# Two transformer blocks on one core: the first stage's order, a shift applied behind a transpose, and two attention heads moved ahead of a projection

## The chip, the core and the metric

The kernel runs as one launch on one core of a Trainium2 chip. The core has five instruction streams, each executed in its own order: TensorE (PE, matrix products and transposes, with PEld for its weight loads), VectorE (DVE), ScalarE (ACT), GpSimd (POOL) and SyncE (SP, which here only issues transfers). Transfers (DMA) are issued by an engine into a queue and moved by 16 shared DMA engines. The metric is the device time of one execution in microseconds (us); lower is better.

## The reference

Two blocks follow each other on 512 tokens of width 1024, in 32-bit floats. What the change touches is the first block's mixer and the start and the second attention of the second block's mixer:

```python
# first block
h = rmsnorm(x, norm1_g[l])
proj = h @ w_in[l]
qa, ka, va, iq, ik, iw, qb, kb, vb, g_lr, r_gate = jnp.split(proj, split_points, axis=-1)
...
o_a = dsa_attention(qa, ka, va, iq..., ik, iw, rel_bias)   # an index score picks 128 keys a query
...
o_b = gla_chunked(...)                                      # gated linear attention
x = x + jnp.concatenate([o_a, o_b], axis=-1) @ w_out[l]
x = x + hier_moe(rmsnorm(x, norm2_g[l]), ...)               # 32 experts
# second block: c gives a shift and a scale, h = rms_norm(x) * g * (1 + scale) + shift
...
proj = h @ w_in
o_mla = causal_block_attention(q_mla, k_mla, v_mla, ...)
o_fox = causal_block_attention(heads(fq), heads(fk), heads(fv), ..., cum_log_f)
...
# then 64 routed experts and a shared one
```

The six vectors of shift, scale and gate come from `silu(c) @ w_mod + b_mod`, `c` being a vector of 1024 numbers and `w_mod` 1024 x 6144. They depend on nothing that the first block computes.

## The kernel before

Tokens lie in four tiles of 128 (`t` or `i`). A product in 32 bits is made of three passes: an operand is split into a high part and a rest (`xh`, `xl`, and `wh`, `wl` for weights, lines 136 and 137), and lines 108 to 110 multiply high by high, high by rest, rest by high. So each chunk of a weight (0.5 MB, `w`, line 130) is loaded by SP, split by ACT (`wh`) and POOL (`wl`), and then read by PE.

A scheduler decides the order of each engine's instructions when the program is built, from the order of the code, from priorities and from hints such as `issue_after`; on the chip that order is fixed.

**First stage** (`phase_a`, the first 330 us). Projections of the first block are made one after another: the index part (`ev_d`), q (`qT`), k (`kT`), then the values (`va`), then those of the linear attention. For q and k each tile is copied out by ACT (line 344, with a square for the norm in line 346), normalised by DVE (line 354, k only), transposed by PE (line 358) and copied back by ACT (line 359). `select(i)` makes the mask of the best keys for tile i: PE makes index scores (`ix`, line 307), ACT takes their positive part (`rl`, line 309), DVE sums them (line 313) and then takes 16 rounds of eight maxima each (lines 319 and 321). The attention heads come in a `front` (scores `qk` in line 379, DVE softmax steps in lines 387 and 389) and a `back` (line 406 transposes, line 415 values), the back `LAG` = 2 pairs of heads behind the front.

Beside this runs `phase_mod`, a generator: the first two of the six vectors of the second block (j = 0 the shift, j = 1 the scale) are computed on PE from `mw`, 1 MB pieces of `w_mod` in two buffers. Each of the four pieces of a j gives eight small products (line 1439); then ACT copies the sum (`macc`) and PE folds it (line 1445), DVE adds the bias (line 1446) and the result is stored in memory (`modD`). `ccol` is silu(c). The bias table of the attention (`brs`, 2.5 MB, issued on ACT's queue) is read back in pieces (`toep`, line 383) on SP's queue.

**Turn to the second block** (`phase_c`, from 630 us). For each half (512 columns) of each token tile DVE computes `h` = x · rs · gs (line 1503), POOL adds the shift, held as a row repeated on 128 partitions (line 1504), PE transposes it (line 1507, `xt`), ACT copies the high part `xh` (line 116) and DVE makes the rest `xl` (line 117). The first projection starts on these parts.

**Second attention of the second block** (`attention(qF, kF, ...)`). Its values `vF` are projected first, then its heads start.

After the first stage and between the mixers stand the expert layers, whose weights (1 MB pieces `wg`, `wu`, `wd`, line 801) are loaded by SP into buffers that come free as the work goes on.

Of the kernel before, what the change touches and what calls it, by code (L numbers as in the profile page):

```python
# [19 lines left out]
NT = 4  # L20
KD = 8
# [33 lines left out]
class K:  # L55
# [84 lines left out]
    def proj(self, pool, xh, xl, segs, evac, kd=KD, wb=2):  # L140

        width = sum(hi - lo for _, lo, hi in segs)
        banks = [self.pbank("pr") for _ in range(NT)]
        for h in range(0, kd, 2):
            nk = min(2, kd - h)
            wh, wl = self.weights(pool, segs, h, nk, 512, wb)
            for t in range(NT):
                ts = slice(t * 128, (t + 1) * 128)
                for j in range(nk):
                    self.mm3(banks[t][:, :width], rows(xh, h + j)[:, ts], rows(xl, h + j)[:, ts], wh[:, j, :width],  # L150
                             wl[:, j, :width], h + j == 0, h + j == kd - 1)
        for t in range(NT):
            evac(t, banks[t])
# [23 lines left out]
ML = 12  # L177
MA = (0, 0, 16, 0)


def phase_a(k, side):
# [321 lines left out]
    def step(n):  # L503
        for _ in range(n):
            next(mod, None)
    k.proj(po, xh, xl, [(w_in, 1536, 1832), (w_in, 2856, 2872)], ev_d)
    step(MA[0])
# [5 lines left out]
    step(MA[1])  # L513
    select(2)
    k.proj(po, xh, xl, [(w_in, 512, 1024)], ev_qk(kT, False))
    with tc.issue_after(act), tc.issue_after(dve), tc.issue_after(k.wloads[ML]):
        step(MA[2])
    select(3)
    k.proj(po, xh, xl, [(w_in, 1024, 1536)], lambda t, b: nc.scalar.activation(va[:, t, :], b, AF.Copy))
    step(MA[3])  # L520
    heads = [(i, hp) for i in range(NT) for hp in range(4)]
    for n in range(len(heads) + LAG):
        if n < len(heads):
            front(*heads[n])
        if n >= LAG:
            i, hp = heads[n - LAG]
            for r in range(2):
                back(i, 2 * hp + r)
    step(16)
# [884 lines left out]
def phase_mod(k, ctx):  # L1414
# [5 lines left out]
    c, _ = mod_col(k, pool)  # L1420
# [5 lines left out]
    nc.gpsimd.tensor_copy(sel, s2[:, :, None].to_broadcast([128, 2, 32]))  # L1426
    wv = I["w_mod_2"][0].rearrange("(p k) n -> p k n", p=128)
# [29 lines left out]
def rows_c(k):  # L1457
# [12 lines left out]
    def load(after):  # L1470
        with k.tc.issue_after(after):
            got.extend(row(k, p, s, n, "r", 3, k.nc.sync) for s, n in
                       ((k.modD[D:2 * D], "gs"), (k.modD[:D], "sh"), (k.I["g_mix_norm_2"][0], "gr")))
# [12 lines left out]
def phase_c(k, rctx, rp, rows):  # L1486
# [12 lines left out]
    for t in range(NT):  # L1499
        h = e.tile([128, D], F32, name="h", bufs=2)  # L1500
        for q in range(2):
            c = slice(q * 512, (q + 1) * 512)
            nc.vector.scalar_tensor_tensor(h[:, c], k.xres[:, t, c], rs4[:, t:t + 1], gs[:, c], op0=ALU.mult, op1=ALU.mult)
            nc.gpsimd.tensor_add(h[:, c], h[:, c], sh[:, c])
            b = k.bank("xt")
            for j in range(4):
                nc.tensor.transpose(b[:, j * 128:(j + 1) * 128], h[:, (4 * q + j) * 128:(4 * q + j + 1) * 128], ident)
            ts = slice(t * 128, (t + 1) * 128)
            k.split(xs[q][0][:, :, ts], xs[q][1][:, :, ts], b.rearrange("p (k s) -> p k s", k=4))
# [182 lines left out]

    def attention(q, kt, v, oT, kd):
        heads = [(i, h) for i in range(NT) for h in range(8)]
        for n in range(len(heads) + 2):
            if n < len(heads):
                front(q, kt, kd, *heads[n])
            if n >= 2:
                back(v, oT, *heads[n - 2])


    oM = a.tile([128, 4, 2, S], F32R, name="oM")
    attention(qM, kM, vM, oM, 96)
    vF = p.tile([128, NT, 512], F32, tag="v", name="vF", bufs=2)
# [329 lines left out]
```

## Time and profile before

| | |
|---|---|
| median of 3 runs (range) | 1698.6 us (1694.95 to 1703.54) |
| the profiled execution | 1696.1 us |
| its span in the trace | 1694.3 us |
| mean granted TensorE clock | 0.963 of full speed |
| PE busy | 1556.0 us, 92% |
| DVE busy | 969.3 us, 57% |
| ACT busy | 540.5 us, 32% |
| POOL busy | 359.0 us, 21% |

Busy shares are averages over stages that have different limits. PE at 92% leaves 138 us in which it waits; where those lie, and what ends each of them, is what the trace has to say.

### The profile page before, as it was taken

What the parts mean: (1) busy time and instruction counts of PE and PEld (TensorE: products, weight loads), DVE (VectorE), ACT (ScalarE), POOL (GpSimd) and SP (SyncE); (2) the same over time, 40 slices, a digit from 0 to 9 for tenths busy, and PEclk for the clock granted to TensorE, in tenths of its full rate; (3) what the DMA queues carried; (4) which work ended last, traced back from release to release, by engine and by line L of the source; (5) the groups of instructions that cost most, each with busy time, mean ns of one, the idle gap of its engine ahead of it and who ended that gap; (6) DMA issues with size and microseconds to landing.
All of it is one profiled execution on the core that took longest, in us unless ns stands there. A gap on an engine that the chain in (4) does not pass through costs nothing.

```text
span 1694.3 us, 28618 instructions
## 1 busy us (share of the span) xinstructions
PE 1556.0 (92%) x10917; PEld 1063.8 (63%) x10917; DVE 969.3 (57%) x2195; ACT 540.5 (32%) x1068; POOL 359.0 (21%) x296
## 2 busy tenths in 40 slices
PE   6789998987999877899999998999999999999996
PEld 5565556774665446675657776865666666666663
DVE  4492875853655346637454535455656656656656
ACT  4431876431211123545562222311112112112112
POOL 2332561012101105331104442113111111011000
PEclk9898999997999997999999999899999999999998
DMA  4526234467999963233005836758999999999961
GB/s 150 179 62 215 74 111 153 190 228 276 417 416 416 418 261 104 71 92 112 26 1 177 255 120 226 290 195 321 378 409 381 400 407 416 422 415 421 415 265 63
DMA packets 103311, 421.30 MB, mean 249 GB/s; under 512 B 22420, under 2 KB 29050, under 8 KB 65796
## 3 DMA queue, kind: packets, MB, share of 16 engines
q1 hardware_dynamic: 81984, 389.77, 59.8%
q0 software_dynamic: 9968, 19.04, 3.1%
q10 hardware_dynamic: 11220, 10.63, 1.9%
q8 instruction: 87, 1.43, 0.3%
q14 instruction: 52, 0.43, 0.1%
HBM read 420.51 MB, written 9.21 MB: 254 GB/s over the span
## 4 chain that ended last, share of the span: by engine, by line
PE 47%; DVE 4%; DMA 3%; POOL 1%; ACT 1%; issue 1%; SPq 0%; DVEq 0%; ACTq 0%; POOLq 0%
PE g L972 8%; PE u L972 8%; PE sc L1050 7%; PE y L996 7%; PE qk L1660 2%; PE ob L1688 2%; DMA mw<-in_w_mod_dram 2%; PE xT L937 2%; PE pt L110 2%; PE pt L109 1%; PE pt L108 1%; PE pt L1680 1%; DVE macc L1399 1%; DMA w<-in_w_in_dram 1%; PE wo L109 1%
## 5 line engine op out<-in xcount | busy, mean ns | idle before, releaser
L137 POOL TENSOR_TENSOR wl<-w,wh 128x1024 fp32r<-128x1024 f32 (+4 forms) x72 | 167.3, 2325 | 384.5 <-ACT wh L136 373.7
L1051 DVE TENSOR_TENSOR xres<-xres,sc 128x512 f32<-128x512 f32 x368 | 224.5, 682 | 4.2 <-PE sc L1050 1.0
L972 PE MATMUL u<-wu,xT 128*32 128x256 f32 (+2 forms) x2240 | 180.3, 388 | 11.9 <-DMA wu<-in_w_exp_up_dram 8.4
L972 PE MATMUL g<-wg,xT 128*32 128x256 f32 (+2 forms) x2240 | 177.2, 383 | 1.3 <-SPq L1143 0.8
L914 POOL DMA_INDIRECT xg<-hD,ii x46 | 46.2, 1004 | 609.3 <-issue 504.4
L996 PE MATMUL y<-wd,hT 128*32 128x512 f32 (+2 forms) x1120 | 167.6, 596 | 0.0
L972 PEld LDWEIGHTS u<-wu,xT 128*32 128x32 f32 (+2 forms) x2240 | 119.9, 121 | 62.1 <-DMA wu<-in_w_exp_up_dram 10.3
L972 PEld LDWEIGHTS g<-wg,xT 128*32 128x32 f32 (+2 forms) x2240 | 104.5, 119 | 85.0 <-issue 33.4
L978 DVE SCALAR_TENSOR_TENSOR hid<-u,gc,hid 128x256 f32<-128x256 f32 x46 | 22.3, 484 | 236.1 <-PE u L972 236.1
L136 ACT ACTIVATE wh<-w 128x1024 fp32r<-128x1024 f32 (+4 forms) x88 | 89.8, 1021 | 196.6 <-PE pt L109 74.2
L1050 PE MATMUL sc<-yh,st 128*128 128x512 f32 x368 | 152.2, 416 | 0.0
L1050 PE MATMUL sc<-yl,st 128*128 128x512 f32 x368 | 144.4, 395 | 0.1
L986 ACT ACTIVATE hT<-hT 128x256 f32<-128x256 f32 x46 | 17.7, 385 | 300.3 <-PE hT L983 300.3
L109 PE MATMUL pr<-wl,xh 128*128 128x512 f32 (+2 forms) x256 | 104.5, 408 | 6.0 <-POOL wl L137 6.0
L116 ACT ACTIVATE yh<-y 128x512 fp32r<-128x512 f32 x92 | 55.0, 597 | 163.0 <-DVE y L1004 110.7
L108 PE MATMUL pr<-wh,xh 128*128 128x512 f32 (+2 forms) x256 | 103.3, 408 | 0.3 <-ACT xh L116 0.3
L996 PEld LDWEIGHTS y<-wd,hT 128*32 128x32 f32 (+2 forms) x1120 | 46.6, 118 | 90.7 <-issue 88.3
L110 PE MATMUL pr<-wh,xl 128*128 128x512 f32 (+2 forms) x256 | 102.9, 403 | 0.3 <-DVE xl L117 0.3
L117 DVE TENSOR_TENSOR yl<-y,yh 128x512 fp32r<-128x512 f32 x92 | 63.7, 692 | 67.1 <-ACT yh L116 55.2
L110 PE MATMUL pt<-xh,wl 128*128 128x512 f32 x224 | 89.3, 400 | 2.1 <-POOL wl L137 2.1
L108 PE MATMUL pt<-xh,wh 128*128 128x512 f32 x224 | 90.1, 402 | 1.1 <-ACT wh L136 0.7
L109 PE MATMUL pt<-xl,wh 128*128 128x512 f32 x224 | 89.0, 397 | 0.0
(533 smaller groups left out, 2832.2 us busy)
## 6 DMA issues: line engine op xcount, KB each, us to landing
wg<-in_w_exp_gate_dram SPq DMA_DIRECT2D x96, 1024.0 KB
wu<-in_w_exp_up_dram SPq DMA_DIRECT2D x96, 1024.0 KB
wd<-in_w_exp_down_dram SPq DMA_DIRECT2D x96, 1024.0 KB
w<-in_w_in_dram SPq DMA_DIRECT2D x52, 512.0 KB
mw<-in_w_mod_dram SPq DMA_DIRECT2D x32, 512.0 KB
mw<-in_w_mod_dram SPq DMA_DIRECT2D x8, 1024.0 KB
w<-in_w_out_dram SPq DMA_DIRECT2D x16, 512.0 KB
brs<-brd ACTq DMA_DIRECT2D x1, 2560.0 KB
```

The source lines that it names most:

```text
L108: nc.tensor.matmul(out, lhsT=lh, rhs=rh, start=first, stop=False)
L109: nc.tensor.matmul(out, lhsT=lh, rhs=rl, start=False, stop=False)
L110: nc.tensor.matmul(out, lhsT=ll, rhs=rh, start=False, stop=last)
L116: hi = nc.scalar.activation(dh, src, AF.Copy)
L117: lo = nc.vector.tensor_sub(dl, src, dh.bitcast(F32))
L136: nc.scalar.activation(wh[:, :, :c], w[:, :, :c], AF.Copy)
L137: (eng or nc.gpsimd).tensor_sub(wl[:, :, :c], w[:, :, :c], wh[:, :, :c].bitcast(F32))
L914: self.gathered = nc.gpsimd.indirect_dma_start(out=x, out_offset=None, in_=src, in_offset=bass.IndirectOffsetOnAxis(ap=ii[:, :1], axis=0), ...
L972: nc.tensor.matmul(b[sl], lhsT=xT[:, kk, sl], rhs=g[h][:, kk], start=kk == 0, stop=kk == KD - 1)
L996: nc.tensor.matmul(b[sl], lhsT=hT[:, j, sl], rhs=d[:, j, h * 512:(h + 1) * 512], start=j == 0, stop=j == 1)
L1050: nc.tensor.matmul(b, lhsT=st[:, ts], rhs=y[h][i], start=i == 0, stop=i == 1)
L1051: nc.vector.tensor_add(self.acc[:, t, hs], self.acc[:, t, hs], b)
```

## The change

Three things are changed.

1. **First stage.** `phase_mod` yields twelve times instead of ten, so that its pieces can be placed one at a time. The load of `c` is issued first of all on ACT's queue, its silu and the three helper tiles come at the very start. One piece of the work on j = 0 is put beside each chunk of the k projection (`beside=`), one piece of j = 1 beside each chunk of the value projection, rather than all ten steps in a block behind the k projection, under a hint that held them back (`ML`, `MA`). The fronts of the first two pairs of heads come ahead of the value projection.
2. **Turn.** The shift is loaded as a tile `shc` of 128 x 8 numbers, one number a partition, rather than as a row of 1024 on every partition. POOL's addition is gone; the shift is added behind the transpose, by ACT as a bias while it copies `xh`, and by DVE inside the operation that makes `xl`. That takes four pieces of 128 columns each, since each has its own eight numbers, where one operation of 512 columns stood.
3. **Second attention.** `ahead` issues the fronts of the first two heads of an attention ahead of its loop; for the second one they now stand ahead of the projection of its values.

```diff
-    def proj(self, pool, xh, xl, segs, evac, kd=KD, wb=2):
+    def proj(self, pool, xh, xl, segs, evac, kd=KD, wb=2, beside=None):
...
+            if beside:
+                beside()
...
+    step(1)
     k.proj(po, xh, xl, [(w_in, 1536, 1832), (w_in, 2856, 2872)], ev_d)
-    step(MA[0])
...
     k.proj(po, xh, xl, [(w_in, 0, 512)], ev_qk(qT, True))
-    step(MA[1])
     select(2)
-    k.proj(po, xh, xl, [(w_in, 512, 1024)], ev_qk(kT, False))
-    with tc.issue_after(act), tc.issue_after(dve), tc.issue_after(k.wloads[ML]):
-        step(MA[2])
+    step(1)
+    k.proj(po, xh, xl, [(w_in, 512, 1024)], ev_qk(kT, False), beside=lambda: step(1))
+    step(1)
     select(3)
-    k.proj(po, xh, xl, [(w_in, 1024, 1536)], lambda t, b: nc.scalar.activation(va[:, t, :], b, AF.Copy))
-    step(MA[3])
     heads = [(i, hp) for i in range(NT) for hp in range(4)]
-    for n in range(len(heads) + LAG):
+    for n in range(LAG):
+        front(*heads[n])
+    k.proj(po, xh, xl, [(w_in, 1024, 1536)], lambda t, b: nc.scalar.activation(va[:, t, :], b, AF.Copy), beside=lambda: step(1))
+    step(1)
+    for n in range(LAG, len(heads) + LAG):
         if n < len(heads):
             front(*heads[n])
...
-    c, _ = mod_col(k, pool)
+    c = pool.tile([128, KD], F32, name="ccol")
+    nc.scalar.dma_start(c, k.I["c_2"][0].rearrange("(p k) -> p k", p=128))
+    yield
+    nc.scalar.activation(c, c, AF.Silu)
...
+            gs = row(k, p, k.modD[D:2 * D], "gs", "r", 3, k.nc.sync)
+            gr = row(k, p, k.I["g_mix_norm_2"][0], "gr", "r", 3, k.nc.sync)
+            sh = p.tile([128, KD], F32, name="shc")
+            k.nc.sync.dma_start(sh, k.modD[:D].rearrange("(k p) -> p k", p=128))
...
-            nc.gpsimd.tensor_add(h[:, c], h[:, c], sh[:, c])
...
-            k.split(xs[q][0][:, :, ts], xs[q][1][:, :, ts], b.rearrange("p (k s) -> p k s", k=4))
+            for j in range(4):
+                hi, s_ = xs[q][0][:, j, ts], sh[:, 4 * q + j:4 * q + j + 1]
+                nc.scalar.activation(hi, b[:, j * 128:(j + 1) * 128], AF.Identity, bias=s_)
+                nc.vector.scalar_tensor_tensor(xs[q][1][:, j, ts], b[:, j * 128:(j + 1) * 128], s_, hi.bitcast(F32),
+                                               op0=ALU.add, op1=ALU.subtract)
...
+    def ahead(q, kt, kd):
+        for n in range(2):
+            front(q, kt, kd, *heads_[n])
...
+    ahead(qM, kM, 96)
     attention(qM, kM, vM, oM, 96)
+    ahead(qF, kF, 66)
     vF = p.tile([128, NT, 512], F32, tag="v", name="vF", bufs=2)
```

How this moves the instructions is seen at three places. The first is ACT's order around the silu of `c`. Before, it stands in the middle of the q projection (`q`, `sq` are its copies and squares, `rl` the index scores):

```order
L1380 DMA ccol<-in_c_dram 128x8
L309 ACTIVATE rl<-ix 128x256 x2
L344 ACTIVATE q<-pr 128x512
L346 ACTIVATE sq<-pr 128x512
L1381 ACT_TABLE_LOAD
L1381 ACTIVATE ccol<-ccol 128x8
L344 ACTIVATE q<-pr 128x512
L346 ACTIVATE sq<-pr 128x512
```

Now it stands at the start of the program, ahead of the squares of the first norm (`va,ss<-xall`), with a table load of its own and one behind it:

```order
L1422 DMA ccol<-in_c_dram 128x8
L199 ACT_TABLE_LOAD
L199 ACTIVATE ss<-ss 128x1
L1424 ACT_TABLE_LOAD
L1424 ACTIVATE ccol<-ccol 128x8
L234 ACTIVATE va,ss<-xall 128x1024
L88 ACT_TABLE_LOAD
L88 ACTIVATE rs1y<-rs1u 128x1
```

Of the q projection's copies nothing stands behind `ccol` any more. The second place is PE's order where the index scores of `select(3)` start (`ix` of 512 columns). Before, they follow the last piece and the fold of j = 1, deep in the projections that come after k (`c_` is the helper tile that holds silu(c)):

```order
L108 MATMUL pr<-wh,xh 128x512
L1439 MATMUL mod<-mw,c_1053 32x512 x4
L109 MATMUL pr<-wl,xh 128x512
L110 MATMUL pr<-wh,xl 128x512
L108 MATMUL pr<-wh,xh 128x512
L109 MATMUL pr<-wl,xh 128x512
L1445 MATMUL mod<-macc,msel 64x512
L307 MATMUL ix<-ikS,iqS 128x512 x3
```

Now they follow the last transposes of the k projection and the fold of j = 0, and the first scores of the heads (`qk`) stand fifteen rows further:

```order
L108 MATMUL pr<-wh,xh 128x512
L358 MATMUL qt<-ident,q 128x128 x4
L1450 MATMUL mod<-macc,msel 64x512
L307 MATMUL ix<-ikS,iqS 128x512 x3
L109 MATMUL pr<-wl,xh 128x512
L307 MATMUL ix<-ikS,iqS 128x512 x2
L110 MATMUL pr<-wh,xl 128x512
L307 MATMUL ix<-ikS,iqS 128x512
L108 MATMUL pr<-wh,xh 128x512
```

What was behind eight pieces of `mw` is now behind four, and 85 rows of PE earlier. The third place is DVE's order at the turn. Before, with `cs` the angles of the rotary embedding:

```order
L1503 SCALAR_TENSOR_TENSOR h<-xres,rs_2781,gs 128x512 x4
L1515 CAST pf<-pi 128x4
L1521 TENSOR_SCALAR cs<-inv,pf 128x16 x3
L117 TENSOR_TENSOR xl<-xt,xh 128x4x128
L1503 SCALAR_TENSOR_TENSOR h<-xres,rs_2781,gs 128x512
L117 TENSOR_TENSOR xl<-xt,xh 128x4x128
L1503 SCALAR_TENSOR_TENSOR h<-xres,rs_2781,gs 128x512
L117 TENSOR_TENSOR xl<-xt,xh 128x4x128 x4
L1503 SCALAR_TENSOR_TENSOR h<-xres,rs_2781,gs 128x512 x2
```

Now, up to the last `h`:

```order
L1511 SCALAR_TENSOR_TENSOR h<-xres,rs_2779,gs 128x512 x4
L1519 SCALAR_TENSOR_TENSOR xl<-xt,shc,xh 128x128
L1511 SCALAR_TENSOR_TENSOR h<-xres,rs_2779,gs 128x512
L1519 SCALAR_TENSOR_TENSOR xl<-xt,shc,xh 128x128 x2
L1511 SCALAR_TENSOR_TENSOR h<-xres,rs_2779,gs 128x512
L1519 SCALAR_TENSOR_TENSOR xl<-xt,shc,xh 128x128 x4
L1511 SCALAR_TENSOR_TENSOR h<-xres,rs_2779,gs 128x512
L1519 SCALAR_TENSOR_TENSOR xl<-xt,shc,xh 128x128 x20
L1511 SCALAR_TENSOR_TENSOR h<-xres,rs_2779,gs 128x512
```

There are 32 pieces of `xl` where eight operations stood, and the angles come behind nearly all of them. On POOL the eight additions are gone, so its next work there is the rests of the weights (`wl`).

## Rows read from the trace of the kernel before

**Rows 1.** The page, busy time of each engine over the span

```profile
PE 1556.0 (92%) x10917; PEld 1063.8 (63%) x10917; DVE 969.3 (57%) x2195; ACT 540.5 (32%) x1068; POOL 359.0 (21%) x296
```

**Rows 2.** PE's waits, 60 to 330 us: waiting line, releaser, us, times, longest

```profile
PE qt L358 <- ACT q L344: 10.0, 3, 5.9
PE mod L1439 <- DMA mw<-in_w_mod_dram: 3.8, 1, 3.8
```

**Rows 3.** PE in order of time, 60 to 83 us: the last of the three

```profile
81.18 0.66 PE L358 MATMUL qt<-ident,q 128*128 128x128 f32 x4 [1.50 <-ACT q L344]
```

**Rows 4.** Busy time by stretch: length, engines (instructions), clock, DMA share, GB/s

```profile
60.00:82.00 22.00, 12.03 (x49) 8.88 (x47) 12.02 (x29) 9.21 (x18) 4.97 (x8) 0.77 0.55 199
82.00:132.00 50.00, 43.72 (x177) 33.59 (x175) 46.39 (x128) 19.94 (x35) 17.02 (x7) 0.90 0.28 78
132.00:170.00 38.00, 34.15 (x156) 18.70 (x155) 5.37 (x11) 7.66 (x11) 7.80 (x4) 0.91 0.61 213
170.00:260.00 90.00, 81.54 (x418) 51.11 (x418) 68.04 (x162) 71.53 (x159) 48.63 (x39) 0.98 0.33 93
...
500.00:600.00 100.00, 91.29 (x797) 54.48 (x794) 44.88 (x97) 15.25 (x30) 13.14 (x10) 0.95 1.01 417
...
640.00:674.00 34.00, 28.70 (x130) 24.67 (x131) 23.46 (x42) 13.25 (x19) 21.11 (x13) 0.80 0.37 99
```

**Rows 5.** ACT in order of time: start, duration, instruction, idle before and releaser

```profile
49.58 0.78 ACTq L223 DMA_DIRECT2D brs<-brd  x1
...
63.30 0.36 ACTq L1380 DMA_DIRECT2D ccol<-in_c_dram  x1
...
69.04 1.28 ACT L1381 ACT_TABLE_LOAD   x1
74.41 0.21 ACT L1381 ACTIVATE ccol<-ccol 128x8 f32<-128x8 f32 x1 [4.08 <-DMA ccol<-in_c_dram]
...
78.61 1.06 ACT L136 ACTIVATE wh<-w 128x1024 fp32r<-128x1024 f32 x1 [3.02 <-DMA w<-in_w_in_dram]
```

**Rows 6.** SP's queue in order of time, 49 to 80 us: first read of the bias table

```profile
74.23 0.34 SPq L383 DMA_DIRECT2D toep<-brs  x1
```

**Rows 7.** DVE in order of time, 128 to 175 us

```profile
135.79 0.36 DVE L332 TENSOR_SCALAR mask<-mask 128x384 f32<-128x384 f32 x1
...
169.15 0.68 DVE L1446 TENSOR_TENSOR mb<-mb,mod 64x512 f32<-64x512 f32 x1 [23.46 <-PE mod L1445]
```

**Rows 8.** A group of instructions, 0 to 300 us: busy, mean ns, idle before

```profile
L1439 PE MATMUL mod<-mw,c 128*32 128x512 f32 x64 | 9.2, 660 | 3.8 <-DMA mw<-in_w_mod_dram 3.8
```

**Rows 9.** SP's queue in order of time, 250 to 300 us: a first expert load

```profile
266.87 0.33 SPq L801 DMA_DIRECT2D wg<-in_w_exp_gate_dram  x1
```

**Rows 10.** PE's waits, 629 to 690 us

```profile
PE xt L1507 <- DMA inv<-in_c_inv_dram: 10.4, 1, 10.4
...
PE xt L1507 <- POOL h L1504: 3.5, 5, 1.4
```

**Rows 11.** DVE and POOL in order of time, 629 to 682 us

```profile
637.84 4.75 DVE L1503 SCALAR_TENSOR_TENSOR h<-xres,rs,gs 128x512 f32<-128x512 f32 x4 [2.35 <-POOL f L1591]
638.67 6.27 POOL L1504 TENSOR_TENSOR h<-h,sh 128x512 f32<-128x512 f32 x4 [1.56 <-DVE h L1503]
...
654.21 1.41 DVE L1503 SCALAR_TENSOR_TENSOR h<-xres,rs,gs 128x512 f32<-128x512 f32 x2
...
659.21 1.28 DVE L117 TENSOR_TENSOR xl<-xt,xh 128x512 fp32r<-128x512 f32 x2
```

**Rows 12.** Groups of instructions, 629 to 700 us, by operand shape: busy, mean ns

```profile
L117 DVE TENSOR_TENSOR xl<-xt,xh 128x512 fp32r<-128x512 f32 x8 | 5.3, 682 | 3.3 <-ACT xh L116 3.2
...
L119 ACT ACTIVATE lh<-lt,gqc 128x128 fp32r<-128x128 f32 x8 | 3.0, 370 | 6.8 <-PE lt L1572 5.9 <-DVE ll L120 0.8
L120 DVE SCALAR_TENSOR_TENSOR ll<-lt,gqc,lh 128x128 fp32r<-128x128 f32 x8 | 2.8, 346 | 0.7 <-ACT lh L119 0.7
```

**Rows 13.** PE's waits, 810 to 850 us

```profile
PE pt L1680 <- DVE se L1667: 1.2, 1, 1.2
```

More of the change, by code (lines that the diff above doesn't have):

```diff
@@ L176 @@
 WV = (1, 1)
-ML = 12
-MA = (0, 0, 16, 0)
 def phase_a(k, side):
@@ L512, in phase_a @@
     k.proj(po, xh, xl, [(w_in, 0, 512)], ev_qk(qT, True))
-    step(MA[1])
     select(2)
-    k.proj(po, xh, xl, [(w_in, 512, 1024)], ev_qk(kT, False))
-    with tc.issue_after(act), tc.issue_after(dve), tc.issue_after(k.wloads[ML]):
-        step(MA[2])
+    step(1)
+    k.proj(po, xh, xl, [(w_in, 512, 1024)], ev_qk(kT, False), beside=lambda: step(1))
+    step(1)
     select(3)
-    k.proj(po, xh, xl, [(w_in, 1024, 1536)], lambda t, b: nc.scalar.activation(va[:, t, :], b, AF.Copy))
-    step(MA[3])
     heads = [(i, hp) for i in range(NT) for hp in range(4)]
-    for n in range(len(heads) + LAG):
+    for n in range(LAG):
[3 more added lines that the diff above has]
+    for n in range(LAG, len(heads) + LAG):
         if n < len(heads):
             front(*heads[n])
[L525 to L529, printed above, removed]
+        i, hp = heads[n - LAG]
+        for r in range(2):
+            back(i, 2 * hp + r)
+    for _ in mod:
+        pass
     mctx.close()
@@ L1426, in phase_mod @@
     nc.gpsimd.tensor_copy(sel, s2[:, :, None].to_broadcast([128, 2, 32]))
+    yield
     wv = I["w_mod_2"][0].rearrange("(p k) n -> p k n", p=128)
@@ L1471, in load @@
         with k.tc.issue_after(after):
-            got.extend(row(k, p, s, n, "r", 3, k.nc.sync) for s, n in
-                       ((k.modD[D:2 * D], "gs"), (k.modD[:D], "sh"), (k.I["g_mix_norm_2"][0], "gr")))
+            gs = row(k, p, k.modD[D:2 * D], "gs", "r", 3, k.nc.sync)
+            gr = row(k, p, k.I["g_mix_norm_2"][0], "gr", "r", 3, k.nc.sync)
+            sh = p.tile([128, KD], F32, name="shc")
+            k.nc.sync.dma_start(sh, k.modD[:D].rearrange("(k p) -> p k", p=128))
+            got.extend((gs, sh, gr))
     def make(after):
@@ L1691, in back @@
             k.split(oT[:, :, 0, ts], oT[:, :, 1, ts], ob.rearrange("p (h t) -> p h t", h=4))
+    heads_ = [(i, h) for i in range(NT) for h in range(8)]
+    def ahead(q, kt, kd):
+        for n in range(2):
+            front(q, kt, kd, *heads_[n])
     def attention(q, kt, v, oT, kd):
[L1694 to L1699, printed above, removed]
+        for n in range(2, len(heads_) + 2):
+            if n < len(heads_):
+                front(q, kt, kd, *heads_[n])
+            back(v, oT, *heads_[n - 2])
     oM = a.tile([128, 4, 2, S], F32R, name="oM")
+    ahead(qM, kM, 96)
     attention(qM, kM, vM, oM, 96)
+    ahead(qF, kF, 66)
     vF = p.tile([128, NT, 512], F32, tag="v", name="vF", bufs=2)
```

## The prediction

> **What bounds the kernel now.** I read the page first: PE is busy for 92% of the span [rows 1], so a change pays where it takes away a wait of PE, or work on PE, and nowhere else. Then I asked for PE's waits and for the busy time by stretch, to see where the other 8% lie. In the first stage PE is busy 12.03 of 22 us between 60 and 82, 43.72 of 50 up to 132, 34.15 of 38 up to 170, and 81.54 of 90 up to 260 [rows 4]. Those stretches have different limits.
>
> From 60 to 82 the limit is one engine waiting on another. PE waits 10.0 us in three pieces, the longest 5.9, for the copy of q by ACT [rows 2]. ACT's order of time tells why: it issues the load of `ccol` at 63.30, and at 74.41 it has stood 4.08 us for it, behind a table load of 1.28; the next copies of q stand behind that. At 78.61 it waits 3.02 us again, for a weight [rows 5]. Both late arrivals have one cause: the bias table was issued at 49.58 [rows 5], and SP's queue reaches its first read-back of it at 74.23 [rows 6]; the weights that stand behind that read-back start only then.
>
> From 82 to 132 DVE is busy 46.39 of 50 us [rows 4], with the selection rounds: DVE sets the pace. From 132 to 170 DVE is busy 5.37 of 38 [rows 4]: after the mask of `select(2)` ends at 135.79 + 0.36 it has only two bias additions of `phase_mod` to do, and idles 23.46 us before the second [rows 7]. The next selection must wait, since its scores are behind the last product of `phase_mod` on PE. PE waits 3.8 us there for one piece of `mw` [rows 2]. From 170 to 260 DVE must then make up: 68.04 of 90 us busy, PE idle for 8.5 [rows 4].
>
> At the turn PE waits 10.4 us for its first transpose and another 3.5, in five pieces, for POOL's additions [rows 10]. (The first is put down to a small load; the order of time shows `h` from DVE at 637.84 and POOL's addition from 638.67, four in 6.27 us [rows 11], so the addition, about 1.6 each, is what comes last.) At the second attention of the second block PE waits 1.2 us [rows 13].
>
> **The change, first stage.** Six terms.
>
> (a) The silu leaves the q projection, and two pieces of `mw` are asked for ahead of it rather than in the middle of the bias table's transfer. Of the 10.0 us of waits, 5.9 and the last, 1.5 [rows 3], go; the first, 2.6 by difference, I leave, since ACT's index scores stand ahead of that copy of q in both orders. The clock is 0.77 over these 22 us [rows 4]; at full speed 12.03 us of work would take up to 2.8 less. Estimate for both together between 5.4 (the 4.08 and the 1.28 of ACT alone) and 10.2; I take −8.
>
> (b) From 82 to 132 DVE sets the pace, and the four pieces of j = 0 now come in here. 64 products took 9.2 us [rows 8], so four pieces, 32 products, cost PE 4.6. PE has 6.3 idle there, so they fit, but a lead of 8 us does not pass through a stretch that is 93% full on DVE. I give back 4, between 1 and 8.
>
> (c) These four pieces are then missing from the work behind 132: −4.6.
>
> (d) The wait of 3.8 for `mw` goes, since the piece is loaded one projection ahead, and with it the clock's dip (0.91 over 38 us with 34.15 busy, up to 3.1 us); I take −4.8, between −3 and −6.9.
>
> (e) DVE's hole, some 33 us, is filled: `select(3)` starts behind the last transposes of k, the heads 15 rows of PE later, where the hole began. The work of DVE from 132 to 260 is 5.37 + 68.04 = 73.4 us [rows 4] and now has the whole 128 us. PE's 8.5 us of idle in 170 to 260 should fall to about 3, what ordinary hand-overs cost: −5.5, between 0 and −7.5.
>
> (f) New costs: at the start ACT gets two more table changes for the silu, 1.28 each [rows 5], covered in part by the loads of the first inputs; and a piece of `mw` beside the k projection may come late. I take +3, between 0 and +8.
>
> Sum: −8 + 4 − 4.6 − 4.8 − 5.5 + 3 = −15.9, call it −16. It reaches the end only if the expert layer moves with it. From 500 to 600 the transfers are at 1.01 of what the queues do and PE is at 91.29 of 100 [rows 4], so that layer is bound by its loads. But its first load, at 266.87 [rows 9], starts when the first stage sets a buffer free, and the later ones when the layer's own work frees theirs, so the whole stream moves. After that PE is full most of the time.
>
> **The change, turn.** POOL's eight additions go, DVE's and ACT's eight operations of 512 columns become 32 of 128 each. The trace has nearly the same small operations elsewhere, with a number a partition: 0.370 us on ACT and 0.346 on DVE, against 0.682 for DVE's 512 columns [rows 12]. So DVE pays 8 x (4 x 0.346 − 0.682) = 5.6 us more at most; `h` pays less, since four of them take 4.75 us beside POOL's additions and two take 1.41 when POOL is mostly quiet [rows 11], 0.48 each, 3.9 over eight. DVE's whole chain is 8 x (0.70 + 1.38) = 16.7 us, which from 637.84 ends at 654.5. Seventeen small operations of the rotary angles stand ahead of the last rest in the new order; at 0.346 each they would bring the end to 660.4, and the last rest now ends at 659.21 + 1.28 = 660.5 [rows 11]. They are 16 or 64 columns wide, so I take half: 657.5. DVE stays ahead of the old time by 3, and it has no addition to wait for. What PE gains: the first transpose comes about 1.7 earlier (one addition, 6.27 / 4 = 1.6), the 3.5 of POOL waits go, and the rests of the weights come earlier because POOL does nothing else; PE is idle 5.3 of 34 us here [rows 4]. I take −6, between 0 (DVE's small pieces pace it) and −8 (some clock back, 0.80 here [rows 4]).
>
> [...]
>
> [...]
>
> The shift's load shrinks from a row on 128 partitions to one of 4 KB, and the whole expert layer lies between it and its use: nothing.
>
> **The change, second attention.** The 1.2 us of wait [rows 13] go, since the softmax of the first two heads runs under the projection of the values: −1, between 0 and −1.2.
>
> **Sum.** −16 − 6 − 1 = −23. Against the profiled execution's own 1696.1 us this is 1673. The median of the runs is 1698.6, 2.5 higher, inside their spread of 8.6; I keep the profiled one as base. A difference below 0.5%, 8.5 us, can't be told from no change.
>
> **The rivals.**
> 1. *All of it comes.* (b) gives back only 1, (d) and (e) reach 5.8 and 7.5, (f) is nothing: −8 + 1 − 4.6 − 5.8 − 7.5 = −25; with −8 and −1 it is −34, 1662. For it: DVE's hole is 33 us long and nothing else is bound there. Against: DVE still has 93% in 82 to 132.
> 2. *The heads stay paced by DVE and ACT.* ACT is busy 71.53 of 90 in 170 to 260 [rows 4], and each head is a chain over three engines. Then (e) is 0 and the 4.6 of (c) turn into waits: −13, 1683.
> 3. *The small pieces pace the turn.* DVE's chain and the angles end where they ended: the turn gives 0, 1679.
> 4. *The expert layer absorbs the first stage.* If its load stream kept its time, only −7 would be left, 1689. For it: the layer is bound by loads. Against: the first of them wait for buffers of the first stage.
> 5. *Slower: the pieces of `mw` stop PE.* Its order is fixed, so a late 1 MB piece beside a projection stops everything behind it. One late piece cost 3.8 us [rows 2], and up to 2.5 of clock with it by (d). Without the allowance in (f) the rest is −25, so from four late pieces on the gain is gone; six would cost 38: +13, 1709. Against: queues are 0.28 and 0.33 busy in 82 to 132 and 170 to 260 [rows 4].
>
> **How the numbers follow.** My forecast has 0.47, the rivals 0.13, 0.18, 0.10, 0.07 and 0.05. Faster by over 0.5% (below 1690 by the profiled time) are the forecast, 1, 3 and most of 2: 0.83. Within 0.5% are 4 and the upper end of 2: 0.12. Slower is 5: 0.05. The range runs from 1658, just below rival 1, to 1691, just above rival 4; outside lie rival 5 and the tails, less than 2 in 10.
>
> **What would show it.** (a) In the profile after, ACT's wait of 4.08 for `ccol` is gone, PE's waits for q between 60 and 82 are below 4 us, the first read-back of the bias table starts near 65. (c) to (e) The index scores of `select(3)` start near 128, not 169; DVE has no hole of over 10 us behind them; the first expert load comes near 250. (f) Waits of PE for `mw` sum to under 3. Turn: no wait of PE for POOL, the last rest 5 us sooner after the first `h`. Attention: no wait of 1.2 at its start. Wrong would be: waits for `mw` of 10 us or more, PE idle as much as before while heads run, or an expert layer that starts earlier and ends at its old time.

## The result, and the profile after

The changed kernel takes 1677.32 us (median of 4 runs, 1674.85 to 1678.45), the one before 1697.52 in the same comparison (4 runs, 1694.95 to 1703.54): 20.2 us less. The ratio on record is 0.9898 (95% interval 0.9862 to 0.9934); the two medians by themselves give 0.9881. Of the kernels timed later, one run of a_only (1802.6 us) and one of no_fox (1702.7) stand over 1.5% above the fastest of their kernel and are left out of the ratios. Forecast were 1673 and 23 less, range 1658 to 1691. The total came out as forecast; three of the terms did not, and some 4 to 5 us came from a place that the forecast did not name.

The page after, the row that answers to [rows 1]:

```profile
PE 1550.9 (93%) x10917; PEld 1060.7 (63%) x10917; DVE 970.1 (58%) x2219; ACT 542.3 (32%) x1090; POOL 347.4 (21%) x287
```

PE does the same 10917 instructions. Its span fell from 1694.3 to 1675.2, by 19.1, its busy time by 5.1, and the mean granted clock rose from 0.963 to 0.971. I put the 5 us of busy time down to the clock; the other 14 are idle time. (The column "clock" below, worked out otherwise, has 7.)

To see where they lie I took the start times of the same PE instruction in both traces and cut the program at eleven of them. Idle is a stretch's length less PE's busy time in it; clock is the sum over 5-us windows of busy time x (1 − granted clock); both were taken for both kernels, and the last three columns show how much of the difference they make, to some 0.2 us.

| stretch, up to | before, us | after, us | difference | idle | clock | rest |
|---|---|---|---|---|---|---|
| first index scores | 47.1 | 52.7 | +5.6 | +5.0 | 0 | +0.6 |
| last transposes of q | 35.5 | 28.6 | −6.9 | −6.3 | −1.1 | +0.5 |
| last transposes of k | 49.3 | 53.1 | +3.8 | +0.8 | −1.4 | +4.4 |
| first decay product of the linear attention (line 458) | 159.4 | 147.6 | −11.8 | −7.4 | −0.4 | −4.0 |
| first expert product | 109.4 | 109.9 | +0.5 | 0 | +0.7 | −0.2 |
| first transpose of the turn | 239.8 | 238.0 | −1.8 | −1.5 | 0 | −0.3 |
| first transpose of the latent (line 1571) | 38.8 | 34.8 | −4.0 | −1.1 | −2.7 | −0.2 |
| first of the up-projection's transposes (line 1608) | 30.4 | 31.9 | +1.5 | −0.2 | +1.7 | 0 |
| last modulation product (line 1408) | 270.0 | 264.5 | −5.5 | −2.8 | −3.2 | +0.5 |
| norm of the second expert layer (line 1870) | 100.9 | 100.3 | −0.6 | −0.4 | −0.9 | +0.7 |
| end | 613.6 | 613.8 | +0.2 | | | |

The first four rows sum to −9.3, where −16 was forecast. The +4.4 and −4.0 of "rest" answer to the four pieces of the modulation that moved from one stretch to the other.

PE's waits from 60 to 320 us, as in [rows 2]:

```profile
PE qt L358 <- DVE q L354: 5.0, 2, 2.8
PE qt L358 <- ACT q L344: 3.5, 2, 3.1
...
PE mod L1444 <- DMA mw<-in_w_mod_dram: 0.3, 1, 0.3
```

The wait for q is 3.5, was 10.0; the one for `mw` is 0.3, was 3.8. Busy time by stretch, as in [rows 4]:

```profile
0.00:60.00 60.00, 41.10 (x218) 34.34 (x219) 23.79 (x61) 27.17 (x54) 16.37 (x18) 1.00 0.51 161
60.00:82.00 22.00, 18.31 (x80) 14.26 (x79) 13.46 (x33) 10.44 (x19) 9.30 (x8) 0.91 0.57 193
82.00:132.00 50.00, 44.86 (x199) 32.10 (x197) 47.14 (x126) 17.58 (x32) 14.33 (x6) 0.94 0.46 148
132.00:170.00 38.00, 35.69 (x167) 20.62 (x167) 33.57 (x84) 20.08 (x50) 12.99 (x11) 1.00 0.40 132
170.00:260.00 90.00, 83.34 (x427) 52.55 (x426) 37.53 (x89) 64.49 (x128) 44.34 (x32) 0.96 0.28 79
```

DVE is busy 33.57 us between 132 and 170, was 5.37: the hole is filled. PE gained 1.5 us of busy time there and 1.8 from 170 to 260.

What had not been seen coming is the start. ACT in order of time:

```profile
2.72 1.28 ACT L1424 ACT_TABLE_LOAD   x1
4.70 0.21 ACT L1424 ACTIVATE ccol<-ccol 128x8 f32<-128x8 f32 x1 [0.70 <-DMA ccol<-in_c_dram]
5.96 1.28 ACT L88 ACT_TABLE_LOAD   x1
14.32 1.06 ACT L234 ACTIVATE va<-xall 128x1024 f32<-128x1024 f32 x1 [2.24 <-DMA xall<-in_x_dram]
15.37 0.28 ACT L88 ACTIVATE rs1y<-rs1u 128x1 f32<-128x1 f32 x2
15.56 0.57 ACT L116 ACTIVATE xh<-xt 128x512 fp32r<-128x512 f32 x1
16.04 0.71 ACT L136 ACTIVATE wh<-w 128x624 fp32r<-128x624 f32 x1
```

The table loads are over by 7.3 and cost little by themselves. But the order was built with them in it. The root of the second tile's norm (line 88) now stands behind the fourth square, which waits at 14.32 for the last tile of x, and not behind the second. So the second tile's transposes (`xt`) come behind the first products, where before they came ahead of them, and PE has nothing to do while it waits for the first split weight `wh`. PE's wait from 0 to 60 us, and the transposes:

```profile
PE pr L108 <- ACT wh L136: 5.2, 1, 5.2
20.98 1.97 PE L240 MATMUL xt<-ident,xn 128*128 128x128 f32 x8 [0.64 <-DVE xn L236]
```

ACT and PE in the kernel before, at the same places:

```profile
11.36 0.20 ACT L88 ACTIVATE rs1y<-rs1u 128x1 f32<-128x1 f32 x1 [0.22 <-DVE rs1u L87]
14.51 0.72 ACT L136 ACTIVATE wh<-w 128x624 fp32r<-128x624 f32 x1
13.78 1.97 PE L240 MATMUL xt<-ident,xn 128*128 128x128 f32 x8 [0.60 <-DVE xn L236]
```

The four squares stand ahead of `wh` in both kernels. The first product comes 1.4 us later (16.80, was 15.40), the transposes that moved behind it add 2.0 and a wait of 0.6, and the waits for the rests `wl` grew by 1.3 (3.0, was 1.7): 5.3 of the 5.6.

At the bias table SP's first read-back comes at 72.00, in a program that is by then 5.6 late, against 74.23 [rows 6]; `select(3)` starts on PE at 135.60, was 169.04 (just behind the fold that the bias addition at 169.15 waited for [rows 7]); the first expert load comes at 260.03, was 266.87 [rows 9]. The forecast had 65, 128 and 250 for these three:

```profile
72.00 0.34 SPq L383 DMA_DIRECT2D toep<-brs  x1
...
260.03 0.41 SPq L802 DMA_DIRECT2D wg<-in_w_exp_gate_dram  x1
```

At the turn, PE's waits from 615 to 690 us, and the groups of small operations:

```profile
PE xt L1514 <- DVE h L1511: 8.6, 1, 8.6
PE lt L1582 <- DVE la L1578: 6.7, 2, 4.7
```

```profile
L1518 ACT ACTIVATE xh<-xt,shc 128x128 fp32r<-128x128 f32 x32 | 9.7, 371 | 14.0 <-DMA w<-in_w_in_dram 5.7 <-DVE xl L1519 5.5 <-PE xt L1514 2.6
L1519 DVE SCALAR_TENSOR_TENSOR xl<-xt,shc,xh 128x128 fp32r<-128x128 f32 x32 | 9.4, 345 | 2.1 <-ACT xh L1518 1.9
```

No transpose waits for POOL any more (for the rests `wl` PE waits 2.4 us in this window, was 0.9), and the small operations take 371 and 345 ns, where 370 and 346 had been read from other lines [rows 12]. The wait for the latent `la`, which comes behind the projection, grew to 6.7; in the kernel before it was

```profile
PE lt L1571 <- DVE la L1567: 5.6, 2, 3.4
```

At the second attention the wait of 1.2 [rows 13] is gone.

### The profile page after: what moved, and what is told of

It reads as the page before. It is cut to its first block, busy times and chain, and to the rows that moved or that the text cites. A ratio compares the mean times of both kernels' runs of the same rounds, so it can differ in the third digit from the quotient of the medians.

```text
span 1675.2 us, 28638 instructions
## 1 busy us (share of the span) xinstructions
PE 1550.9 (93%) x10917; PEld 1060.7 (63%) x10917; DVE 970.1 (58%) x2219; ACT 542.3 (32%) x1090; POOL 347.4 (21%) x287
## 4 chain that ended last, share of the span: by engine, by line
PE 46%; DVE 5%; DMA 4%; POOL 1%; ACT 1%; issue 1%; SPq 0%; DVEq 0%; ACTq 0%; POOLq 0%
PE g L973 8%; PE u L973 8%; PE sc L1051 7%; PE y L997 7%; PE qk L1671 2%; DMA mw<-in_w_mod_dram 2%; PE ob L1699 2%; PE xT L938 2%; PE pt L110 1%; PE pt L109 1%; PE pt L108 1%; PE pt L1691 1%; DVE macc L1400 1%; POOL wl L137 1%; DMA gmr<-in_g_ffn_norm_dram 1%
```

## The experiments

Each kernel was timed beside the kernel before on the same chip; the kernel before has medians of 1689.4, 1692.9 and 1695.0 us on the three chips used, so ratios are compared, not times. "Ahead" and "late" refer to the same PE instruction in two traces.

### One part of the change at a time

**p1_first**, **p2_turn**, **p3_fox**: before with part 1, 2 or 3 of the diff above alone.

> The kernel before with the first stage's part of the change alone. If the parts add up as they show in the two traces (the first stage ends 9.3 us earlier in the one after, and the expert layer passes on 8.8), the time is about 9 us below before, and no stage behind the expert layer gains. If the 3.4 us that the trace after gains late in the second block (gate stage) come from this part, by loads that start earlier, it is 12 below. If the first stage's gain rests on the other parts, under 5.

> The kernel before with the turn's part alone. Adding up: 4 to 5 us below before, with PE waiting about 2 less for its first transpose and none for POOL. If the small pieces pace the turn, nothing. If the row of the shift that is no longer loaded is what frees a buffer for the late modulation loads, the gate stage gains here as well: 7 to 8 in all.

> The kernel before with the two heads ahead of the value projection alone. The predicted 1.0 to 1.5 us below before, which lies inside what one timing can tell; in the trace the wait of 1.2 at the start of that attention is gone and the following stages are early by that much and no more.

| kernel | median, us (runs) | ratio to before | 95% interval |
|---|---|---|---|
| p1_first | 1687.89 (12) | 0.9955 | 0.9925 to 0.9986 |
| p2_turn | 1707.69 (12) | 1.0051 | 1.0014 to 1.0088 |
| p3_fox | 1693.43 (12) | 0.9984 | 0.9958 to 1.0009 |

The first stage's part does in its trace what it does in the whole: the expert layer starts 9.2 us ahead, and it is passed on. The turn's part, which gains 4 us, made the kernel slower. Its times lie between 1686.6 and 1711.8, nine of twelve above 1706. Its trace is ahead of before by 6.5 us at 820 us and behind by 13.0 at 880. Busy time by stretch, two stretches of the second attention:

```profile
780.00:825.00 45.00, 44.89 (x282) 28.13 (x281) 21.60 (x55) 24.97 (x61) 2.39 (x1) 1.00 0.03 6
825.00:872.00 47.00, 45.76 (x159) 26.27 (x158) 18.76 (x62) 17.72 (x62) 2.37 (x1) 0.56 0.06 18
```

The second row has the granted clock (the number ahead of the last two) at 0.56, and PE gets through 159 instructions where before, p1_first, no_first and after, at 1.00, get through 267 to 290 in as long. By 5-us windows it is at 0.50 from 835 to 870, and at 0.53 in the window on either side. The fall begins some 2 us behind the end of PE's only wait there (at 828.4), the very one that the change's third part removes (its waits from 810 to 880 us):

```profile
PE pt L1686 <- DVE se L1673: 1.2, 1, 1.2
```

That is a rival no step of the prediction had. In before the same wait stands at 833.66, in p1_first one of 1.20 at 822.7, and neither trace has a fall behind it (p1_first is at 1.00 from 825 to 872); but 5 of the 29 runs of before in that comparison are above 1705. Before, from its wait on:

```profile
833.00:880.00 47.00, 45.72 (x275) 26.53 (x273) 29.92 (x88) 28.16 (x89) 1.64 (x1) 1.00 0.04 12
```

### Is it that wait?

**no_fox** is after with part 3 undone; **no_first** is p2_turn with part 3 added, so that each of the two pairs differs in part 3 alone. Of each edit the lines that move work are shown; the rest rewrites the loop.

```diff
# no_fox, against after
...
-    ahead(qF, kF, 66)
     vF = p.tile([128, NT, 512], F32, tag="v", name="vF", bufs=2)
...
# no_first, against p2_turn
...
+    ahead(qF, kF, 66)
     vF = p.tile([128, NT, 512], F32, tag="v", name="vF", bufs=2)
```

> The kernel after with its third part undone: the projection of the values of the second attention stands ahead of its first two heads again. Theory A: PE's wait of 1.2 us at the start of that attention is a place at which TensorE's clock can fall to half for the 40 us that follow (it did so in the profile of the turn's part alone, where it cost some 19 us); then the times have two heaps, one about 2 us above after, near 1680, and one near 1697, and the profile of a run of the second heap shows a granted clock of 0.5 from the start of that attention. Theory B: the fall in that profile came from something else; then all runs lie within 4 us of after.

> The kernel before with the turn's and the second attention's part, without the first stage's. If parts add up: 4 (turn) + 3 (attention and what follows) below before, near 1688, and by theory A no run near 1707, as the turn's part alone has. By theory B a heap near 1707 stays.

| kernel | parts | runs, us | ratio to before |
|---|---|---|---|
| p2_turn | 2 | 1686.6, 1696.1, 1702.6, nine from 1706.9 to 1711.8 | 1.0051 |
| no_first | 2, 3 | twelve from 1678.0 to 1687.7 | 0.9963 (0.9941 to 0.9986) |
| no_fox | 1, 2 | 1673.0, 1676.2, ten from 1689.3 to 1702.7 | 1.0004 (0.9972 to 1.0035) |
| after | 1, 2, 3 | four from 1674.9 to 1678.5 | 0.9898 (0.9862 to 0.9934) |

Both pairs say the same: without part 3 most runs are some 15 to 20 us longer, with it none is. The profile of no_fox has the clock at 0.53 from 816 to 863; that of no_first, in the answering stretch, is at 1.00:

```profile
816.00:863.00 47.00, 45.88 (x159) 26.61 (x160) 17.88 (x59) 15.62 (x55) 0.86 (x1) 0.53 0.04 12
```

```profile
822.00:869.00 47.00, 46.69 (x282) 28.22 (x280) 28.38 (x82) 27.73 (x86) 2.82 (x2) 1.00 0.08 23
```

So theory A holds as far as it says that the lost time hangs on this place and that part 3 keeps it away. That the wait itself brings the clock down, and not something else in the order that part 3 changes, is not shown: the fall follows the wait in both traces that have it, but before and p1_first have the wait without the fall. Why the fall is common with the turn's part (21 of 24 runs of p2_turn and no_fox at 1689 or more) and rarer without it stays open: the wait is 1.2 us in all four traces, and in the 45 us ahead of it PE is busy 44.89 in before and in p2_turn alike.

### The start

**silu_late** holds the silu behind ACT's last copy of the first norm; **mw_late** holds the first pieces of weight on SP's queue behind the index part's weights; **both_late** does both.

```diff
# silu_late, against after
-    step(1)
+    with tc.issue_after(act):
+        step(1)
     k.proj(po, xh, xl, [(w_in, 512, 1024)], ev_qk(kT, False), beside=lambda: step(1))
...
# mw_late, against after
+    def held():
+        with tc.issue_after(k.wloads[7]):
+            step(1)
...
-    k.proj(po, xh, xl, [(w_in, 512, 1024)], ev_qk(kT, False), beside=lambda: step(1))
+    k.proj(po, xh, xl, [(w_in, 512, 1024)], ev_qk(kT, False), beside=held)
```

> The kernel after, with the silu of c held behind the last copy of the first norm on ACT; its 1 MB pieces of weight stay where they are. Theory A: the index part is 5.6 us late in the trace after because the silu's table loads move ACT's order, so that all four squares stand ahead of the first copy; then PE's wait of 5.2 for the first split weight goes and the time is 5 to 6 us below after, near 1672. Theory B: the early 1 MB piece and the other added loads delay the third and fourth tile of x, and ACT's order only follows; then the time stays within 2 us of after.

> The kernel after, with the two first pieces of the modulation's weight held on SP's queue behind the weights of the index part; the silu stays at the start. The silu held back alone brought the index part 4.1 us forward of the 5.6 that it is late. Theory A (ACT's order): the index part stays 5 to 6 us late, since ACT's order at the start is unchanged. Theory B (the added load at the start): it comes 3 us or more forward. If both count, 1 to 2.

> The kernel after, with both held back: the silu behind the last copy of the first norm, the pieces of weight behind those of the index part. The index part should start within 0.7 us of before (47 us), and the first stage end 5 to 7 us ahead of after. In the time 3 to 6 us below after, if the second block does not take it back.

| kernel | first index scores | first expert product | span of its profile | ratio to before |
|---|---|---|---|---|
| before | 47.1 | 400.7 | 1694.3 | |
| after | 52.7 | 391.9 | 1675.2 | 0.9898 |
| mw_late | 52.2 | 388.2 | 1673.4 | 0.9917 (0.9880 to 0.9953) |
| silu_late | 49.6 | 384.5 | 1672.9 | 0.9893 (0.9850 to 0.9937) |
| both_late | 48.2 | 388.1 | 1676.1 | 0.9903 (0.9869 to 0.9936) |

The places speak for ACT's order: with the silu held back the index scores come 3.1 of the 5.6 us sooner (the expectation of mw_late had read 4.1), with the pieces alone 0.5, with both 4.5. The 0.5 is nothing: p1_first, no_fox and turn_big, which have after's first stage, start them between 52.1 and 53.2. But theory A named the wrong wait. In silu_late `wh` starts at 16.34, later than in after, and PE still waits 3.3 us for it; what came back is the place of the second tile, whose transposes now stand ahead of that wait:

```profile
11.87 1.97 PE L240 MATMUL xt<-ident,xn 128*128 128x128 f32 x8 [0.60 <-DVE xn L236]
```

In the time nothing of it is left. The three that hold something back are 4 to 7 us ahead of after at the first expert product and between 2.3 ahead and 0.9 behind at the end. Much of that lead is the scatter of single traces: no_fox and turn_big, with after's first stage, are there at 388.3 and 388.6, so that only silu_late is ahead of them, by 4. What is lost behind lies at several places: silu_late is 8.3 ahead of after within the first expert layer and 6.1 at its end (its loads bound it: 1.01 in [rows 4]), then loses 4 more between 920 and 1060, at PE's wait for the modulation (2.2 in it, 1.4 in after) and in dips of the clock. both_late lost 4.9 us of clock while the heads ran, after 3.4. These dips move from kernel to kernel and are as large as the gain.

### What the early silu was worth, and what the pieces

**a_only** is before with one step of the first part: the load of `c` and the silu at the start. All pieces of weight stay where before has them.

```diff
# a_only, against before
+    step(1)
     k.proj(po, xh, xl, [(w_in, 1536, 1832), (w_in, 2856, 2872)], ev_d)
...
+    step(1)
     k.proj(po, xh, xl, [(w_in, 512, 1024)], ev_qk(kT, False))
-    with tc.issue_after(act), tc.issue_after(dve), tc.issue_after(k.wloads[ML]):
-        step(MA[2])
+    with tc.issue_after(dve), tc.issue_after(k.wloads[12]):
+        step(10)
```

> The kernel before with one step of the first stage's part alone: the load of c and its silu at the start; the eight pieces of weight stay where before has them, in a block behind the k projection, and on SP's queue ahead of the bias table's read-back. ACT's wait of 4.1 and the table load leave the q projection, but the bias table still shares the queues with two pieces, so SP reaches the read-back near where it did (plus the start's delay) and the late weight of that place stays late. Expected: start +5.6, between the index part and the last q transposes -3 to -5 (against -6.9 in after), then as before: the first stage ends 0 to 3 us later than before.

1697.21 us, ratio 1.0022 (0.9994 to 1.0050): no gain. From the index scores to the last transposes of q it takes 34.2 us, before 35.5, after 28.6. PE's waits there (51 to 87 us), ACT's and SP's rows, and last the issue of the bias table in after:

```profile
PE qt L358 <- ACT q L344: 9.0, 3, 8.0
```

```profile
54.31 0.77 ACTq L223 DMA_DIRECT2D brs<-brd  x1
81.04 1.06 ACT L136 ACTIVATE wh<-w 128x1024 fp32r<-128x1024 f32 x1 [6.24 <-DMA w<-in_w_in_dram]
```

```profile
76.79 0.34 SPq L383 DMA_DIRECT2D toep<-brs  x1
```

```profile
55.18 0.77 ACTq L223 DMA_DIRECT2D brs<-brd  x1
```

With the silu gone from the q projection ACT waits 6.24 us for the weight behind the read-back, where it had waited 4.08 for `ccol` and 3.02 for that weight [rows 5]. The stall moved to what was late behind it. What is left of the first part here is the place of the two pieces of weight: in a_only and before SP asks for them between the issue of the bias table and its read-back, and the read-back comes 22.5 and 24.7 us behind the issue; in after they are asked for ahead of it, and it comes 16.8 behind. So the pieces, taken out of the bias table's transfer, together with the silu gave the 6.9 us; the pieces without the silu were not tried.

### The hole of DVE

**late_select** is after with `select(3)` and the first fronts put behind the value projection and the last piece of the modulation.

```diff
-    select(3)
     heads = [(i, hp) for i in range(NT) for hp in range(4)]
-    for n in range(LAG):
-        front(*heads[n])
     k.proj(po, xh, xl, [(w_in, 1024, 1536)], lambda t, b: nc.scalar.activation(va[:, t, :], b, AF.Copy), beside=lambda: step(1))
     step(1)
+    select(3)
+    for n in range(LAG):
+        front(*heads[n])
```

> The kernel after with select(3) and the first two fronts put behind the value projection and the last piece of the modulation. If the filled hole of DVE (forecast at 5.5 us, with up to 7.5) carries the first stage's gain, DVE idles again after select(2) and the time is 5 to 9 us above after. If the pieces' new places and the shorter wait at the bias table carry it, it stays within 3 us.

1671.63 us, ratio 0.9905 (0.9873 to 0.9937): as after. Its `select(3)` starts at 150.07 instead of 135.60, and DVE idles again:

```profile
133.35 0.35 DVE L332 TENSOR_SCALAR mask<-mask 128x384 f32<-128x384 f32 x1
135.19 0.68 DVE L1451 TENSOR_TENSOR mb<-mb,mod 64x512 f32<-64x512 f32 x1 [1.48 <-PE mod L1450]
150.18 0.68 DVE L1451 TENSOR_TENSOR mb<-mb,mod 64x512 f32<-64x512 f32 x1 [14.31 <-PE mod L1450]
```

From the last transposes of k to the first decay product it takes 145.3 us, after 147.6, with 7.3 of idle (8.3) and no clock lost (3.4); no_fox, with after's first stage, takes 146.2 there. So 14.3 us of the 33 can be open again at no cost: PE has enough projections to do meanwhile, and DVE catches up.

**best** joins late_select with both_late.

> The kernel after with silu and pieces held back and with select(3) and the first fronts put behind the value projection. If the gains of the two runs before add up (6 from the start, 2.9 from the late selection, whose trace has no fall of the clock while the heads run), the first stage ends 8 us ahead of after and the time is 4 to 8 us below it. If the fall of the clock in after was chance, only the start's 4 to 6 remain.

1675.22 us, ratio 0.9906 (0.9873 to 0.9938). It is 5.4 ahead of after at the first decay product (2.1 ahead of no_fox) and 0.9 ahead at the norm of the second expert layer. No kernel of these beats after by anything that can be measured.

### The price of the small pieces

**turn_big** has one copy and one subtraction of 512 columns at the turn, and the shift nowhere.

```diff
-            for j in range(4):
-                hi, s_ = xs[q][0][:, j, ts], sh[:, 4 * q + j:4 * q + j + 1]
-                nc.scalar.activation(hi, b[:, j * 128:(j + 1) * 128], AF.Identity, bias=s_)
-                nc.vector.scalar_tensor_tensor(xs[q][1][:, j, ts], b[:, j * 128:(j + 1) * 128], s_, hi.bitcast(F32),
-                                               op0=ALU.add, op1=ALU.subtract)
+            k.split(xs[q][0][:, :, ts], xs[q][1][:, :, ts], b.rearrange("p (k s) -> p k s", k=4))
```

> The kernel after with one copy and one subtraction of 512 columns a half tile at the turn, as before, and no addition of the shift anywhere: the shift is left out, so the output lacks it. If the 32 small operations have a price on the path, PE reaches the end of the first projection 1 to 4 us sooner than in after; if DVE and ACT have the slack that the prediction gave them, within 1 us of after.

Its whole time, 1712.62 us, says nothing of the turn: without the shift the second expert layer's tokens are other ones, and that layer takes some 39 us longer. Up to there it can be read. From the turn's first transpose to the first of the latent it takes 31.5 us, after 34.8; to the up-projection 30.4 more, after 31.9. PE's waits there:

```profile
PE xt L1514 <- DVE h L1511: 8.8, 2, 8.6
PE lt L1578 <- DVE la L1574: 4.9, 2, 2.7
```

The wait for the latent is 4.9 against 6.7 in after. So with the 32 small pieces the path is 3.3 us longer, 2.5 of them idle time, and 1.5 more by a dip of the clock behind the longer wait (0.66 over 665 to 670 us in after, none in turn_big). Three more kernels with the small pieces, no_fox, late_select and mw_late, take 34.9 to 36.4 and 31.9 to 32.3 us in the two stretches.

Not all of the 3.3 is the pieces' own time. The latent's norm on DVE begins with `jk` (line 1573), and in after this falls beside a rest of a weight on POOL; POOL and DVE in order of time:

```profile
655.73 2.35 POOL L137 TENSOR_TENSOR wl<-w,wh 128x1024 fp32r<-128x1024 f32 x1 [4.94 <-ACT wh L136]
656.10 2.40 DVE L1573 TENSOR_TENSOR jk<-la 128x384 f32<-128x384 f32 x1 [3.07 <-ACT la L1570]
659.34 0.54 DVE L1573 TENSOR_TENSOR jk<-la 128x384 f32<-128x384 f32 x1
```

The same operation takes 0.54 us with POOL quiet. In turn_big its first one took 1.36, in before 2.10. I put the 1.0 us between 2.40 and 1.36, out of the 3.3, down to where `wl` falls; another order on POOL was not tried.

## Why the prediction was right, and where it was not

**(a) Right in size, wrong in part of its cause.** −8 was taken, −6.9 measured. Its lower bound, "the 4.08 and the 1.28 of ACT alone", was no bound: a_only takes these away and gains 1.3. The late weight stood right behind and took their place. What (a) names next, the pieces out of the bias table's transfer, is what made it pay.

**(b) and (c) Right.** +4 and −4.6 were taken; the stretch grew by 3.8, with 4.4 more work, and the later one has 4.0 less.

**(d) and (e) Too large.** −4.8 and −5.5 were taken, −7.8 measured for both (7.4 of idle, 0.4 of clock). (d)'s wait fell from 3.8 to 0.3, so it paid about 3.5 and its clock little: after has its own dip, 0.56 and 0.76 in the windows from 190 to 200. The step that failed is in (e): "PE's 8.5 us of idle in 170 to 260 should fall to about 3". DVE's hole is filled, as said, but late_select opens 14.3 us of it again and loses nothing. The 3 was the author's estimate; no run shows it: PE is idle 6.7 of 90 there in after, in hand-overs of 1.7 and less. What of the 7.4 came from filling the first 19 us of the hole was not tried apart.

**(f) Too small.** +3 was taken, +5.6 measured, inside the bounds (0 to +8), but not by the cost named. Two table changes were priced by their duration; silu_late shows that it is their place in the order that costs, since ACT's order at the start was built around them and puts the second tile's root behind a wait for the last tile of x. Rival 5, late pieces of `mw`, did not come: they cost 0.3. (It counts 2.5 us of clock a piece where (d) has up to 3.1, and its −25 is −26; neither matters here.)

**The expert layer** passed the gain on, as said: ahead by 8.8 at its first product, by 8.8 at its last. Rival 4 did not come.

**Turn: −6 taken, −4.3 measured** (−1.8, −4.0, +1.5; 2.8 of it idle time). The first transpose came 1.8 sooner, where 1.7 was taken. The price of each small operation was right to the nanosecond or two. What failed is "DVE stays ahead of the old time by 3". In after the last rest ends 23.6 us behind the first `h`, in before 22.7 [rows 11]: DVE and ACT hand the last pieces to each other one by one, with the angles between. PE could do most of the projection in that time, and the loss appears one step on, as the longer wait for the latent. Rival 3, small pieces that pace the turn, is half right: up to 3.3 us of the possible gain, and 1.5 of clock. turn_big shows this price on PE's path; on DVE four operations of 345 ns stand where one of 682 stood [rows 12].

`h` took 2.74 us for four without POOL's additions beside it, against 4.75 with them [rows 11]. In after POOL does nothing from 628.30 to 633.35:

```profile
629.03 2.74 DVE L1511 SCALAR_TENSOR_TENSOR h<-xres,rs,gs 128x512 f32<-128x512 f32 x4 [2.35 <-POOL f L1602]
```

Beside the rests of the weights (`wl`, two from 633.35 to 638.15) one `h` took 0.75 us at 633.13 and one 1.45 at 634.83, against 0.74 at 631.95 with POOL quiet. So it is longer beside POOL in some places and not in others; what decides this was not tried.

**Second attention: −1 taken, −1.5 measured** in the trace. The term missed what the part is worth: without it most runs with the turn's part are some 15 to 20 us longer, with the clock at 0.56 and 0.53 behind that wait in the two that were profiled, and the whole change ends where it began (no_fox, 1.0004).

**Not forecast: some 4 to 5 us** between 780 and 1040: a dip of the clock that before has at 780 to 790 and after has not (1.6 us), and at 950 a shorter wait for the modulation and another dip (3.3 us together). That wait is between 1.4 and 3.9 us in the six traces of before, after, the single parts and silu_late, with no order to it, so this is likelier chance of the two profiles than a gain. Without it the terms sum to −15, not −19; yet the four runs of after lie within 3.6 us of each other. One trace gives such terms to some 3 us only: the same first stage ends 3.2 to 3.6 us sooner in no_fox and turn_big than in after, and 0.4 in p1_first. At −15 the forecast of −23 would still have been inside its range, but 8 us off. That the total was nearer than its terms is luck.

## What to carry to other kernels

Where one engine waits twice in a row for late transfers, taking the first wait away can move the stall to the second (in a_only 6.24 us, where before had 4.08 and 3.02): look for what both have in common, here the bias table's transfer, read back 22.5 and 24.7 us behind its issue with two pieces of weight asked for in between, and 16.8 with them ahead of it. A small instruction that is hoisted to the start is priced by the order that the scheduler builds around it, not by its duration: here two table loads of 1.28 us, over by 7.3, and the index scores 5.6 us late, 3.1 of which came back with the silu held. Parts of a change need not add: one that lengthens no wait can still come with a fall of the clock at a wait that was there already (p2_turn: 1.2 us of wait as in before, and 0.56 behind it). Time each part alone and each with one undone, and look at the granted clock where the traces part.

## What the runs showed of the hardware that was not expected

In p2_turn and no_fox a stretch of some 44 us at a granted clock of 0.50 by 5-us windows (0.56 and 0.53 over 47 us) began about 2 us behind a wait of PE of 1.2 us. PE was busy 45.8 and 45.9 of the 47 us and got through 159 instructions instead of 267 to 290; the loss in those traces was about 21 us. The same wait stood in before and p1_first with the clock at 1.00 behind it. While heads of attention ran, PE's work thus stayed at 0.50 although PE hardly paused; what began and what ended it was not tried.

In after two operations of DVE took a multiple of their time beside one of POOL. `jk`, above, ended 0.4 us behind the end of `wl`, at four times its own time. An operation of 128x2 numbers (line 95) took 2.20 us from 661.84, beside a `wl` from 661.65 to 664.02, and 0.17 at 665.32 with POOL quiet. Both stand on the path to the latent, and before has them too (2.10 and 2.19 us), so that by an estimate, (2.40 − 0.54) + (2.20 − 0.17), up to some 4 us may be had there by another order on POOL; it was not tried.
